# Four groups of in-place sums moved from a doubled loop into the product behind it

## The chip, the cores and the metric

The kernel runs on one core of a Trainium2 chip. The metric is the device time in microseconds (us) of one execution; the median of several runs is compared.

## What is computed

One decoder layer on a residual stream x of 1024 rows by 1024 columns in float32: a mixer (differential attention beside a short convolution, one projection in, one out), a layer norm, and a gated feed-forward part with a hidden width of 2816, with a second layer norm at the end. The part that matters here is the last product, the down projection, and its layer norm:

```python
def conv_glu(x, w_up, conv_w, conv_b, w_down):
    up = jnp.einsum('bsd,df->bsf', x, w_up)
    g, val = up[..., :D_FF], up[..., D_FF:]
    g = causal_dwconv(g, conv_w) + conv_b
    return jnp.einsum('bsf,fd->bsd', jax.nn.silu(g) * val, w_down)
...
        f = conv_glu(h, ffn_w_up[l], ffn_conv_w[l], ffn_conv_b[l], ffn_w_down[l])
        h = layer_norm(DEEPNORM_ALPHA * h + f, ln2_g[l], ln2_b[l])
```

## The kernel before

Every float32 operand of a matmul is split into a high part and a remainder. ScalarE casts the high part (L60), VectorE subtracts it from the operand (L61), and TensorE makes three products of 128x128 by 128x512: high by high (L69), high by low (L70), low by high (L71). In the trace the activations' operand is S and the weights' operand is T.

The down projection multiplies 1024 x 2816 activations by 2816 x 1024 weights. Both are cut in two along each side, and seven products of half blocks take the place of eight; sums of blocks are formed before some of the products. One product has 11 slices of the hidden width (HK = 11) and four blocks of 128 rows, so one slice is 4 x 3 = 12 matmuls, called a step here. X (dx in the trace) and Z (dz) are four accumulators each.

The order of the work:

1. The doubled loop, `for j in range(HK + 2)`, makes two products at once. At each j it does slice j of a11 by b11 into X, and slice j - 2 of (a21 + a22) by (b12 - b11) into Z. The two sums for Z are made by `add` (L802, on VectorE) into temporary tiles tm. When X is complete, `first_add` (L808) brings its four row blocks into the residual r11 (rw in the trace).
2. In the same loop, from j = 3 on, `thirds(j - 3)` overwrites four tiles of slice j - 3 with the sums that later products want: a21 becomes a11 - a21, a11 becomes a22 - a21 (the new one), b12 becomes b22 - b12, b11 becomes b12 + b11. These are four `add` of 128x512 on VectorE, also L802. The call for slice 10 stands behind the loop.
3. The third product, `product(X, a11, b11, ...)`, multiplies the new a11 and b11 into X. `product` makes the operands of slice i, then its 12 matmuls, then calls `after[i]` if there is one, then, for i in 0 and 1, two of the jobs in `owed` (here `first_add` of Z into r22, four in all).
4. Four more products follow in the same way, then the layer norm of the last rows.

The operand tiles S and T come from a ring of seven tiles, so a cast into a tile of the ring waits until the matmuls of the tile's former contents are over. The instructions of an engine run in the order in which the program puts them on that engine; that order is set when the program is built, it mostly follows the text, and an instruction whose inputs are ready early can stand ahead of one that is written before it.

Of the kernel before, what the change touches and what calls it, by code (L numbers as in the profile page):

```python
# [31 lines left out]
NEARLY = 4  # L32
FIN = 5
OWED = (0, 1)
POOL_LO = (2, 3, 4, 5, 6)
REUSE = 2
RMS_AT = [(c, 1) for c in range(4)]
# [6 lines left out]
def layer_kernel(ctx: ExitStack, tc: tile.TileContext, x, xt, w_in, w_v, lam, vecs, w_out, ln, w_up, w_down, out):  # L44
# [461 lines left out]
    def bank(name):  # L506
        return p8.tile([P, 512], F32, name=name, tag="b", bufs=8)
# [61 lines left out]
    def weights(t0, k, eng):  # L569
        raw = e0.tile([P, D], F32, name=f"wo{t0}_{k}_r", tag="wg", bufs=NWG)  # L570
        SQ.dma_start(raw, w_out[k * P:(k + 1) * P, :])
        wo = [e0.tile([P, 2, 512], F32R, name=f"wo{t0}_{k}_{d}", tag="ring", bufs=RING[0]) for d in range(2)]
        for d in range(2):
            split(wo[d][:, 0, :], wo[d][:, 1, :], raw[:, d * 512:(d + 1) * 512], eng=eng)
        return wo

    pending, late, held = [], [], {}
    for t0 in (0, 3, 6):
# [4 lines left out]
        for ki, k in enumerate(order):  # L583
            if ki < REUSE and t0:
                wo = held[k]
            else:
                wo = weights(t0, k, G if ki in POOL_LO and t0 == 6 else None)
            held[k] = wo
# [49 lines left out]
    def wgate(f):  # L638
        return wload8(f, "wg", NWG)
# [3 lines left out]
    for f in range(NEARLY):  # L643
        if f >= NEARLY - 2:
            turn(*rows_[f - NEARLY + 2])
        wg, X, Y = wgate(f), bank(f"X{f}"), bank(f"Y{f}")
# [19 lines left out]
    HK = NF // 2  # L666
# [4 lines left out]
    def operand(src, which, i, tail=False, eng=None):  # L671
        if tail and not (which == "T" and i < HK - NTAIL + RT):
            v = ep.tile([P, 2, 512], F32R, name=f"{which}{i}", tag="ra", bufs=NF - NKEEP)
        else:
            v = e0.tile([P, 2, 512], F32R, name=f"{which}{i}", tag="ring", bufs=RING[0])
        split(v[:, 0, :], v[:, 1, :], src, eng=eng)
        return v

    act, b11, ready = [], [], []
    for f in range(NF):  # L680
        if f in early:
            wg, X, c11 = early[f]
        else:
            wg, X, c11 = wgate(f), bank(f"X{f}"), None
# [69 lines left out]
    a11, a21 = [act[k][:, c0] for k in half1], [act[k][:, c1] for k in half1]  # L754
    a12, a22 = [act[k][:, c0] for k in half2], [act[k][:, c1] for k in half2]

    def residual(half, cols_, tiles):
        for t in range(4):
            SQ.dma_start(tiles[t], h1_d[4 * half + t][:, cols_])
        return tiles  # L760

    def rtiles(name, tag, bufs):
        return [ep.tile([P, 512], F32, name=f"{name}_{t}", tag=tag, bufs=bufs) for t in range(4)]
# [3 lines left out]
    def mm_row(ps, op, t, first, last):  # L767
        s_, t_ = op
        ts = slice(t * P, (t + 1) * P)
        mm3(ps[t], s_[:, 0, ts], s_[:, 1, ts], t_[:, 0, :], t_[:, 1, :], first, last, skip_group_check=True)  # L770

    def product(ps, sa, tb, first, ntail=0, done=None, after={}, prompt=False):
        ops = []

        def mms(i, t):
            mm_row(ps, ops[i], t, first and i == 0, i == HK - 1)
            if i == HK - 1:
                if ntail or prompt:
                    done(t)
                else:  # L780
                    owed.append(lambda: done(t))

        for i in range(HK):
            tail = i >= HK - ntail
            ops.append((operand(sa(i), "S", i, tail), operand(tb(i), "T", i, tail)))
            if not tail:
                for t in range(4):
                    mms(i, t)
            if i in after:
                after[i]()  # L790
            if i in OWED:
                for _ in range(2):
                    if owed:
                        owed.pop(0)()
        for t in range(4):
            for i in range(HK - ntail, HK):
                mms(i, t)

    def add(x_, y_, op, out=None):
        if out is None:  # L800
            out = ep.tile([P, 512], F32, name="tm", tag="r", bufs=4)
        V.tensor_tensor(out, x_, y_, op=op)  # L802
        return out
# [3 lines left out]
    def first_add(r, ps):  # L807
        return lambda t: V.scalar_tensor_tensor(r[t], r[t], ALPHA, ps[t], op0=ALU.mult, op1=ALU.add)  # L808

    def finish(t, r0, r1):  # L810
        mv = e1.tile([P, 2], F32, name="mv", tag="mv", bufs=3)
        V.bn_aggr(mv, st[t])
        ve = e1.tile([P, 1], F32, name="ve", tag="ve", bufs=3)
        G.tensor_scalar(ve, mv[:, 1:2], EPS, None, op0=ALU.add)
        rs = e1.tile([P, 1], F32, name="rs", tag="rs", bufs=3)
        G.tensor_tensor(rs, ve, mhalf, op=ALU.pow)
        for r, g, c in ((r0, g2[0], c0), (r1, g2[1], c1)):
            V.scalar_tensor_tensor(r, r, mv[:, 0:1], g, op0=ALU.subtract, op1=ALU.mult)
        for r, bb, c in ((r0, b2[0], c0), (r1, b2[1], c1)):
            V.scalar_tensor_tensor(r, r, rs, bb, op0=ALU.mult, op1=ALU.add)  # L820
            SQ.dma_start(out[t * P:(t + 1) * P, c], r)

    X = [bank(f"dx{t}") for t in range(4)]
# [3 lines left out]
    r22 = residual(1, c1, [r[:, 1, :] for r in rw])  # L827


    def thirds(i):  # L830
        add(a11[i], a21[i], ALU.subtract, a21[i])
        add(a22[i], a21[i], ALU.subtract, a11[i])
        add(b22[i], b12[i], ALU.subtract, b12[i])
        add(b12[i], b11[i], ALU.add, b11[i])

    for j in range(HK + 2):
        if j < HK:
            op = ready.pop(0) if ready else (operand(a11[j], "S", j), operand(b11[j], "T", j))
            for t in range(4):
                mm_row(X, op, t, j == 0, j == HK - 1)  # L840
        if j >= 2:
            i = j - 2
            op = (operand(add(a21[i], a22[i], ALU.add), "S", i),
                  operand(add(b12[i], b11[i], ALU.subtract), "T", i))
            for t in range(4):
                mm_row(Z, op, t, i == 0, i == HK - 1)
            if j >= HK:
                for t in (0, 1) if j == HK else (2, 3):
                    first_add(r11, X)(t)
        if j >= 3:  # L850
            thirds(j - 3)
    thirds(HK - 1)
    for t in range(4):
        owed.append(lambda t=t: first_add(r22, Z)(t))

    r12 = residual(0, c1, rtiles("r12", "r", 4))

    product(X, lambda i: a11[i], lambda i: b11[i], False, done=first_add(r12, X))

    def done_p3(t):  # L860
        V.tensor_tensor(r12[t], r12[t], Z[t], op=ALU.add)
# [17 lines left out]
    def done_p7(t):  # L879
# [4 lines left out]
            after={FIN + t: (lambda t=t: finish(t, r11[t], r12[t])) for t in range(4)})  # L884
# [51 lines left out]
```

## Time and profile before

| what | value |
|---|---|
| median of 3 runs | 1144.28 us |
| lowest of 3 runs | 1142.41 us |
| profiled execution, its time | 1145.87 us |
| profiled execution, its span | 1143.5 us |
| TensorE busy | 1090.8 us, 95% of the span |
| VectorE busy | 914.4 us, 80% |
| ScalarE busy | 522.5 us, 46% |
| granted TensorE clock, mean | 0.986 of full speed |
| doubled loop and third product on TensorE | 912.46 to 1015.02 us |

The highest of the three runs, 2755.74 us, stands alone; the median is not moved by it.

The times in the rows below are microseconds from the start of the span. In the rows PE is TensorE, PEld its weight load, DVE VectorE, ACT ScalarE, POOL GpSimd. A matmul's duration reaches over the start of the next one, since they are pipelined; the pace is the distance of the starts. The same holds for the instructions of VectorE and ScalarE.

### The profile page before, as it was taken

How to read it: one execution, taken by the hardware profiler on the slowest of the kernel's cores; microseconds unless marked ns; L12 is line 12 of the kernel's file. 1: busy time of each engine (PE TensorE's matmuls, PEld its weight loads, DVE VectorE, ACT ScalarE, POOL GpSimd, SP SyncE). 2: the span in 40 equal slices, each digit the busy share in tenths (PEclk: the TensorE clock that was granted, in tenths of full speed). 3: DMA queues.
4: the chain of work that ended last, by engine and by line, in shares of the span. 5: the costliest groups of instructions: out<-in, count | busy, mean ns of one | idle time of the engine just before them, and what ended most of it. 6: DMA issues, size and time to landing. Idle time of an engine off the chain costs nothing.

```text
span 1143.5 us, 13823 instructions
## 1 busy us (share of the span) xinstructions
PE 1090.8 (95%) x4924; PEld 876.7 (77%) x4924; DVE 914.4 (80%) x1377; ACT 522.5 (46%) x980; POOL 174.6 (15%) x198
## 2 busy tenths in 40 slices
PE   7899999999999999789999999999999999899997
PEld 5676777877768888568888888888888887688885
DVE  7858889779887788998967676767677599977697
ACT  5347677377676334434433434343434243344450
POOL 4501313113032214760000000000000000000102
PEclk9899999999999999999999999999999999999999
DMA  7430121211205764423232222222222393111111
GB/s 257 136 111 26 42 82 41 86 60 47 79 28 172 263 203 164 152 74 111 94 109 75 92 74 93 74 93 73 93 74 74 121 411 139 37 62 40 38 74 73
DMA packets 50276, 118.51 MB, mean 104 GB/s; under 512 B 5024, under 2 KB 18464, under 8 KB 50208
## 3 DMA queue, kind: packets, MB, share of 16 engines
q1 hardware_dynamic: 50208, 117.64, 29.8%
q8 instruction: 38, 0.62, 0.2%
q14 instruction: 30, 0.25, 0.1%
HBM read 90.88 MB, written 26.74 MB: 103 GB/s over the span
## 4 chain that ended last, share of the span: by engine, by line
PE 67%; DVE 17%; ACT 6%; DMA 5%; POOL 3%; issue 2%; POOLq 0%; DVEq 0%; SPq 0%; ACTq 0%
PE X L71 8%; PE X L69 8%; PE X L70 8%; PE Z L70 5%; PE Z L71 5%; PE Z L69 5%; PE dx L70 3%; PE dx L71 3%; PE dx L69 3%; PE op L71 2%; PE op L70 2%; PE op L69 2%; DVE a L61 2%; PE dz L70 2%; PE dz L71 2%
## 5 line engine op out<-in xcount | busy, mean ns | idle before, releaser
L61 DVE TENSOR_TENSOR a<-s,a 128x512 fp32r<-128x512 f32 x118 | 85.4, 725 | 45.1 <-ACT a L60 44.1
L60 ACT CAST a<-s 128x512 fp32r<-128x512 f32 x118 | 73.4, 623 | 94.8 <-PE X L71 42.7
L60 ACT CAST a<-w 128x512 fp32r<-128x512 f32 x106 | 66.0, 623 | 87.4 <-PE X L71 40.7
L61 DVE TENSOR_TENSOR a<-w,a 128x512 fp32r<-128x512 f32 x102 | 71.4, 701 | 21.6 <-ACT a L60 21.2
L60 ACT CAST T<-b 128x512 fp32r<-128x512 f32 x66 | 40.7, 622 | 72.1 <-PE dz L71 35.6
L70 PE MATMUL dx<-T,S 128*128 128x512 f32 x176 | 69.8, 397 | 3.6 <-DVE T L61 3.6
L71 PE MATMUL dx<-T,S 128*128 128x512 f32 x176 | 69.4, 395 | 0.0
L69 PE MATMUL dx<-T,S 128*128 128x512 f32 x176 | 67.3, 390 | 0.0
L61 DVE TENSOR_TENSOR T<-b,T 128x512 fp32r<-128x512 f32 x66 | 45.4, 690 | 24.1 <-ACT T L60 24.1
L687 POOL MEMSET gs<- 128x2 f32 x22 | 2.2, 100 | 379.2 <-DVE t L706 379.2
L71 PE MATMUL op<-wo,cl 128*128 128x512 f32 x128 | 51.4, 402 | 4.5 <-DVE cl L61 4.5
L422 DVE TENSOR_REDUCE nm<-sc 128x1 f32<-128x128 f32 (+5 forms) x64 | 47.6, 751 | 7.6 <-PE sc L421 7.1
L69 PE MATMUL dz<-T,S 128*128 128x512 f32 x132 | 49.2, 401 | 3.8 <-ACT T L60 3.7
L70 PE MATMUL dz<-T,S 128*128 128x512 f32 x132 | 52.2, 396 | 0.0
L71 PE MATMUL dz<-T,S 128*128 128x512 f32 x132 | 51.9, 393 | 0.0
L69 PE MATMUL op<-wo,ch 128*128 128x512 f32 x128 | 51.4, 402 | 0.0
L70 PE MATMUL op<-wo,ch 128*128 128x512 f32 x128 | 51.0, 399 | 0.0
L426 ACT ACTIVATE p<-sc,nm 128x128 f32<-128x128 f32 (+5 forms) x64 | 47.6, 746 | 7.3 <-DVE p L435 4.1
L707 ACT ACTIVATE t<-t 128x1024 f32<-128x1024 f32 x22 | 23.4, 1062 | 51.2 <-DVE t L706 51.2
L344 POOL TENSOR_TENSOR me<-me,y 128x256 f32<-128x256 f32 x16 | 12.6, 786 | 217.9 <-ACT y L343 217.9
L419 PE MATMUL sc<-k,q 128*128 128x512 f32 (+2 forms) x96 | 37.2, 394 | 7.3 <-ACT p L426 6.1
L60 ACT CAST wo<-wo_r 128x512 fp32r<-128x512 f32 x40 | 24.4, 620 | 41.0 <-PE op L71 37.8
(312 smaller groups left out, 3415.3 us busy)
## 6 DMA issues: line engine op xcount, KB each, us to landing
w<-in_w_up SPq DMA_DIRECT2D x44, 512.0 KB, 3.3
b<-in_w_down SPq DMA_DIRECT2D x44, 256.0 KB, 6.8
w<-in_w_in SPq DMA_DIRECT2D x20, 512.0 KB, 3.5
wo_r<-in_w_out SPq DMA_DIRECT2D x20, 512.0 KB, 5.4
act_d<-act SPq DMA_DIRECT2D x19, 512.0 KB, 2.6
ra<-act_d SPq DMA_DIRECT2D x19, 512.0 KB, 7.1
v_d<-vs SPq DMA_DIRECT2D x16, 256.0 KB, 2.7
vhl<-v_d SPq DMA_DIRECT2D x8, 512.0 KB, 4.7
```

The lines of the kernel that those rows point to most:

```text
L60: A.copy(hi, src)
L61: (eng or V).tensor_tensor(lo, src, hi.bitcast(F32), op=ALU.subtract)
L69: T.matmul(ps, lh, rh, start=first, stop=False, **kw)
L70: T.matmul(ps, lh, rl, start=False, stop=False, **kw)
L71: T.matmul(ps, ll, rh, start=False, stop=last, **kw)
L344: G.tensor_tensor(me, me, y, op=ALU.mult)
L419: T.matmul(sc[:, bs], q2[m][:, qs], k2[m][:, bs], start=True, stop=False)
L422: V.tensor_reduce(nm[:, m:m + 1], sc[:, :n], axis=AX.X, op=ALU.max, negate=True)
L426: A.activation(pt[:, :n], sc[:, :n], AF.Exp, bias=nm[:, m:m + 1], accum_out=sm[:, m:m + 1])
L687: G.memset(gs[:, 0:2], 0.0)
L707: A.activation(t_, t_, AF.Silu)
```

## The change

The call of `thirds` in the doubled loop is limited to slices 0 to 6. Those of slices 7, 8, 9 and 10 are given to the third product as `after`, behind its steps 0, 2, 4 and 6. What is computed is the same.

```diff
+NTHIRD = 7
...
     def thirds(i):
         add(a11[i], a21[i], ALU.subtract, a21[i])
         add(a22[i], a21[i], ALU.subtract, a11[i])
...
-        if j >= 3:
+        if 3 <= j < NTHIRD + 3:
             thirds(j - 3)
-    thirds(HK - 1)
     for t in range(4):
         owed.append(lambda t=t: first_add(r22, Z)(t))
 
     r12 = residual(0, c1, rtiles("r12", "r", 4))
 
-    product(X, lambda i: a11[i], lambda i: b11[i], False, done=first_add(r12, X))
+    product(X, lambda i: a11[i], lambda i: b11[i], False, done=first_add(r12, X),
+            after={2 * i: (lambda i=i: thirds(NTHIRD + i)) for i in range(HK - NTHIRD)})
```

## Rows read from the trace of the kernel before

**Rows 1.** The page, first part: busy time, share and instructions of each engine.

```profile
PE 1090.8 (95%) x4924; PEld 876.7 (77%) x4924; DVE 914.4 (80%) x1377; ACT 522.5 (46%) x980; POOL 174.6 (15%) x198
```

**Rows 2.** Windows: busy time of each engine by stage, granted clock, DMA share, GB/s.

```profile
core 0: us, PE busy (x) PEld busy (x) DVE busy (x) ACT busy (x) POOL busy (x), PEclk, DMA share, GB/s
915.00:985.00 70.00, 62.58 (x260) 48.98 (x259) 69.59 (x116) 27.14 (x48) 0.00 (x0) 0.97 0.61 239
985.00:1015.00 30.00, 30.00 (x128) 24.66 (x127) 24.73 (x41) 11.43 (x20) 0.00 (x0) 0.95 0.03 10
1015.00:1045.00 30.00, 30.00 (x134) 24.83 (x133) 23.18 (x39) 12.56 (x22) 0.00 (x0) 1.00 0.27 87
1045.00:1075.00 30.00, 30.00 (x134) 24.86 (x133) 18.82 (x31) 12.58 (x22) 0.00 (x0) 1.00 0.04 12
1075.00:1105.00 30.00, 30.00 (x134) 24.60 (x133) 29.54 (x52) 18.62 (x33) 5.72 (x8) 1.00 0.26 94
```

**Rows 3.** Waits, 900 to 1020, TensorE: total us, times, longest us.

```profile
PE dz L69 <- ACT T L60: 3.7, 2, 2.2
PE dx L70 <- DVE T L61: 3.6, 1, 3.6
```

**Rows 4.** Timeline, TensorE: start, us, instruction, count, idle before and its releaser.

```profile
912.46 0.39 PE L69 MATMUL dx<-T,S 128*128 128x512 f32 x1
...
967.94 0.39 PE L71 MATMUL dz<-T,S 128*128 128x512 f32 x1
970.56 1.97 PE L69 MATMUL dz<-T,S 128*128 128x512 f32 x4 [2.23 <-ACT T L60]
...
976.58 1.20 PE L69 MATMUL dz<-T,S 128*128 128x512 f32 x4 [1.42 <-ACT T L60]
...
979.80 0.84 PE L69 MATMUL dx<-T,S 128*128 128x512 f32 x3
984.27 0.74 PE L70 MATMUL dx<-T,S 128*128 128x512 f32 x1 [3.64 <-DVE T L61]
...
987.79 0.39 PE L69 MATMUL dx<-T,S 128*128 128x512 f32 x1
...
1015.02 0.39 PE L69 MATMUL dz<-T,S 128*128 128x512 f32 x1
...
1134.98 0.39 PE L71 MATMUL dx<-T,S 128*128 128x512 f32 x1
```

**Rows 5.** Timeline, VectorE, around the moved sums (966.08: group 7; 982.32: end of 10).

```profile
965.48 0.69 DVE L61 TENSOR_TENSOR T<-tm,T 128x512 fp32r<-128x512 f32 x1
966.08 0.70 DVE L802 TENSOR_TENSOR ra<-ra 128x512 f32<-128x512 f32 x1
...
968.49 0.70 DVE L802 TENSOR_TENSOR tm<-ra,ra 128x512 f32<-128x512 f32 x1
969.09 0.69 DVE L802 TENSOR_TENSOR tm<-b,b 128x512 f32<-128x512 f32 x1
969.69 0.69 DVE L808 SCALAR_TENSOR_TENSOR rw<-rw,dx 128x512 f32<-128x512 f32 x1
...
982.32 0.70 DVE L802 TENSOR_TENSOR b<-b,b 128x512 f32<-128x512 f32 x1
982.92 0.70 DVE L61 TENSOR_TENSOR S<-act,S 128x512 fp32r<-128x512 f32 x1
983.52 0.70 DVE L61 TENSOR_TENSOR T<-b,T 128x512 fp32r<-128x512 f32 x1
984.12 1.30 DVE L808 SCALAR_TENSOR_TENSOR rw<-rw,dz 128x512 f32<-128x512 f32 x2
...
990.72 0.70 DVE L802 TENSOR_TENSOR act<-ra,act 128x512 f32<-128x512 f32 x1
```

**Rows 6.** Timeline, ScalarE: two casts and what they waited for.

```profile
969.22 0.62 ACT L60 CAST S<-tm 128x512 fp32r<-128x512 f32 x1 [4.12 <-DVE tm L802]
...
980.00 0.62 ACT L60 CAST T<-b 128x512 fp32r<-128x512 f32 x1 [0.87 <-PE dz L71]
```

## The prediction

> **What bounds the kernel now.** The page's first part gives TensorE 95% of the span and VectorE 80% [rows 1]: TensorE is the bound as a mean, and the question is where it is not. The windows by stage answer it [rows 2]. In the doubled loop (915 to 985) VectorE is busy 69.59 of 70.00 us and TensorE only 62.58; in the third product (985 to 1015) TensorE is busy all 30.00 and VectorE 24.73. So the loop is paced by VectorE and what follows it by TensorE. The waits of TensorE say the same: its pauses end on a cast (L60) that had waited for VectorE, or on a remainder of VectorE itself (L61) [rows 3].
>
> How much TensorE loses there comes from its timeline [rows 4]. From 987.79 on the third product runs without a pause: 120 matmuls up to 1015.02, 27.23 us, so 0.227 us each and 2.72 us for a step (one slice, 12 matmuls). The 33 steps of X, Z and the third product begin at 912.46; without loss they would end at 912.46 + 33 x 2.723 = 1002.3. They end at 1015.0, so **12.7 us are lost**: pauses of 2.23, 1.42 and 3.64 us, two stretches in which matmuls are slower right after a pause (eight from 984.27 to 987.79 take 3.52 instead of 1.81 us, 1.7 lost; four L69 at 970.56 take 1.97 instead of the 1.20 at 976.58, and that stretch loses about as much), and about 2 us of small waits. From 1015.02 the other four products are 44 steps, 119.8 us, up to 1134.8; the last matmul starts at 1134.98 [rows 4]. After the third product nothing is lost, and whatever it ends earlier the end should be earlier too.
>
> **What the change moves.** Groups 7 to 10 of the in-place sums, four sums each, leave the loop and stand behind steps 0, 2, 4 and 6 of the third product. No instruction is added or removed. In the trace group 7 holds VectorE from 966.08 to the next instruction at 968.49 [rows 5]: 2.41 us, 0.602 a sum. The four groups are 16 sums, **9.6 us**. The first begins at 966.08 and the last, the sixteenth, at 982.32, all ahead of the low parts of the third product's first slice, for which TensorE waits 3.64 us. The sums issue no transfer, so no DMA and nothing in SP's queue moves. They do not use ScalarE or GpSimd.
>
> **The loop after the change.** Up to 965.48 nothing differs. Then I let VectorE's instructions follow in the order of the trace, 0.60 us each. The two sums for Z's slice 9 start at 966.08 and 966.68 instead of 968.49 and 969.09, X's first residual fills the place that it fills now, the remainders start at 967.88 and 968.48. A cast begins 0.04 us after its sum has ended (968.49 + 0.69 to 969.22) [rows 5, 6], so the casts are over at 967.4 and 968.0. Slice 8 of Z leaves TensorE at 968.2, slice 9 can begin at once; its low part is there at 969.25 (0.2 us late), it ends at 971.1. Slice 10: sums at 969.68 and 970.28, casts over at 971.0 and 971.6, TensorE begins at 971.7 and gets the low part at 972.85, so it waits 0.6 and 0.25 and ends at 974.7. Without loss this would be 972.4: the loop still loses 2.3 us, half of it before 968 where nothing changes. Both slow stretches go with the pauses ahead of them.
>
> **The third product after the change.** VectorE does the last residual of X at 972.68, then the remainders of slice 0 at 973.28 and 973.88: TensorE goes from the loop into step 0 without a pause, up to 977.4. Now program order puts group 7 (974.5 to 976.9), two residuals of Z, remainders of slice 1 (978.08 and 978.68), two residuals, slice 2 (980.48 and 981.08), group 8 (to 984.1), slices 3 and 4, group 9, slices 5 and 6, group 10, slice 7. Today the residuals stand between slices 0 and 1 in just this way (984.12) [rows 5]. Where TensorE is short of a low part it does the four high products of the step first (the rows L69 x4), 0.9 us. So step 1 begins at 977.4, has its four high products done at 978.3 and waits for the low part until 979.45: **1.2 us**. Step 2 does not wait (981.85 against 982.2). Step 3 waits from 984.9 to 985.45: **0.6 us**. From step 4 on VectorE is ahead, since two steps want 4 remainders and one group, 4.8 us, in 5.44 us of TensorE. The casts are no limit: T's third slice waits for Z's last matmul, as now at 980.00 [rows 6], and each later one for the step three before it. Steps 4 to 10 run through, 987.3 + 19.1 = 1006.3.
>
> **The sum:** 1015.0 - 1006.3 = **8.7 us gained**; 2.3 + 1.2 + 0.6 = 4.1 of the 12.7 lost remain. The profiled execution took 1145.87 us with a span of 1143.5, so 1137.2 and 1134.8 after; the runs' median is 1144.28, 1.6 below that execution, and 1144.28 - 8.7 = **1135.6**.
>
> Costed at nothing: the 11 sums for the next product, with which VectorE now fills its free time from 990.7 on [rows 5], start later, about 997. The cover is the free time behind: VectorE is busy 23.18 of 30 us in the next stage and 18.82 of 30 in the one after it [rows 2], 18 us free, against 9.6 us moved. The stage from 1075 has no room (29.54 of 30); if it had to take all of the 9.6 us, the gain would be gone, but 18 us of room lie ahead of it. The last product's sums (L802 on b) follow in the same free time.
>
> Bounds of what the trace does not show. The order inside the third product: if the remainders of slices 1 and 3 come ahead of the groups, both waits fall away, gain 10.4; if TensorE takes the matmuls by row instead of the high products first, each wait starts 0.7 us earlier, gain 8.0. Nothing lost at all would be 12.7. I take program order with the high products first, because both stand so in the rows of now.
>
> **Does TensorE's clock fall in the new pauses?** After the pause of 1.42 us before 976.58 the matmuls are at full speed (2.4 GHz), after those of 2.23 and 3.64 us at half (1.2 GHz) [rows 4]. My longest pause, 1.2 us, is below the first, so I count nothing. The Trainium skill (TensorE: Matmul & The Clock Gate, A second HAM failure mode: psum-queue depth-cycling) says that frequent short idle gaps between groups of matmuls can make the clock go back and forth, and that throughput is lost at each return. The pause of 976.58 does not bear it out here; by that rule the sum would be 7.0.
>
> **The rivals.**
> 1. The clock falls once in the third product. For it: waits of 1.2 and 0.6 us lie 4 us apart, behind 0.6 in the loop. Against it: the row at 976.58. Price 1.7 us (the eight matmuls from 984.27): 7.0 gained, 1137.3; with both waits longer by 0.7, 5.6, 1138.7. Chance 0.15.
> 2. The change does not do what it says: VectorE's order is not strictly that of the text (X's residual of 969.69 stands ahead of remainders that are written before it), and the moved sums could fill the loop's gaps again. For it: their inputs are ready in the loop. Against it: in the rows of now group 7 stands in its place, behind the remainder of 965.48 [rows 5], and a gap between sum and remainder takes one instruction that the residuals already fill. If three of four groups stay in the loop, 9.6 / 4 = 2.4 us gained, 1141.9; chance 0.07.
> 3. Slower: VectorE paces the third product. Each of the four groups stands in front of remainders that TensorE wants next; if every one stalls it in full and the clock falls each time, that is 4 x (2.41 + 1.7) = 16.4 against 12.7 - 2.3 = 10.4 won in the loop: 6.0 slower, 1150.3. It decides from 10.4 us of pauses on. Against it: 4.8 us of work for 5.44 us, and casts that may run three steps ahead. Chance 0.04.
>
> The forecast with its own range (8.0 to 12.7 gained, 1131.6 to 1136.3) has 0.74. Undisturbed single times lie 1.9 below and 1.6 above the median; with that at both ends, and with rival 1 taken in (1131.6 - 1.9 and 1138.7 + 1.6), the range is 1129.7 to 1140.3, and leaves out rivals 2 and 3 and little more. A measurement of this kernel can tell about 2% (23 us) from no change. All that is lost in the stage is 12.7 us, so no case reaches 2% faster, and the slower rival gives 0.5%: faster 0.01, within 2% 0.97, slower 0.02.
>
> **What would show it.** Right: the third product's last matmul ends near 1006 and all later rows are some 9 us earlier; the half-speed matmuls near 970 and 984 are gone; 16 sums stand between the third product's remainders. Wrong step: a pause over 2 us in the third product with half-speed matmuls behind it (rival 1); sums of groups 7 to 10 ahead of slice 0's remainders (rival 2); pauses in steps 1, 3, 5 and 7 (rival 3); pauses from 1060 on would mean that the room behind did not cover the moved work.

## The result, and the profile after

The changed kernel takes 1134.02 us (median of 4 runs, 1133.13 to 1136.27) against 1144.03 us before; the ratio is 0.992, with a 95% interval of 0.9899 to 0.9941. A second measurement, the run `after_again` below, gives 1134.32 us (6 runs) against 1143.32 us, ratio 0.9926, interval 0.9914 to 0.9937. So the change saves 9 to 10 us. It is clear of zero and far inside 2%. The profiled execution took 1134.1 us, its span is 1132.3 us.

The change shifts the lines of the code by one: L70, L71 and L72 are now the three matmuls (high by high, high by low, low by high), L61 the cast, L62 the remainder, L803 the sums and L809 the residuals.

The windows of the changed kernel, by the same stages as [rows 2] (columns as there):

```profile
915.00:985.00 70.00, 68.30 (x291) 53.46 (x290) 69.97 (x117) 29.19 (x52) 0.00 (x0) 1.00 0.57 224
985.00:1015.00 30.00, 30.00 (x134) 24.82 (x133) 29.84 (x51) 12.63 (x23) 0.00 (x0) 1.00 0.14 45
1015.00:1045.00 30.00, 30.00 (x134) 24.86 (x133) 23.52 (x39) 12.65 (x23) 0.00 (x0) 1.00 0.16 53
1045.00:1075.00 30.00, 30.00 (x134) 24.85 (x133) 20.49 (x36) 14.84 (x27) 3.30 (x5) 1.00 0.11 36
1075.00:1105.00 30.00, 30.00 (x132) 24.35 (x131) 30.00 (x50) 15.05 (x27) 2.42 (x4) 1.00 0.18 70
```

From 915 to 985 TensorE is busy 68.30 us instead of 62.58 and makes 291 matmuls instead of 260, at full granted clock (1.00, before 0.97), while VectorE is as busy as it was. The third product has moved ahead, so groups 7 and 8 now lie just before 985 (971.86 to 981.47) and groups 9 and 10 behind it; from 985 to 1015 VectorE is busy 29.84 us instead of 24.73, and TensorE does not pause there.

The waits of TensorE, 900 to 1130, changed kernel (total us, times, longest us), beside [rows 3]:

```profile
PE dx L71 <- DVE T L62: 1.2, 2, 0.9
PE dz L70 <- ACT T L61: 0.4, 1, 0.4
```

And its timeline, the rows that answer to [rows 4]:

```profile
909.82 0.39 PE L70 MATMUL dx<-T,S 128*128 128x512 f32 x1
...
965.53 1.17 PE L70 MATMUL dz<-T,S 128*128 128x512 f32 x4
...
969.12 1.21 PE L70 MATMUL dz<-T,S 128*128 128x512 f32 x4 [0.42 <-ACT T L61]
...
972.37 0.39 PE L70 MATMUL dx<-T,S 128*128 128x512 f32 x1
...
974.86 1.07 PE L70 MATMUL dx<-T,S 128*128 128x512 f32 x4
976.81 0.50 PE L71 MATMUL dx<-T,S 128*128 128x512 f32 x1 [0.88 <-DVE T L62]
...
978.76 1.07 PE L70 MATMUL dx<-T,S 128*128 128x512 f32 x4
...
981.48 1.07 PE L70 MATMUL dx<-T,S 128*128 128x512 f32 x4
982.82 0.50 PE L71 MATMUL dx<-T,S 128*128 128x512 f32 x1 [0.28 <-DVE T L62]
...
984.80 0.39 PE L70 MATMUL dx<-T,S 128*128 128x512 f32 x1
...
1003.85 0.39 PE L70 MATMUL dz<-T,S 128*128 128x512 f32 x1
...
1123.81 0.39 PE L72 MATMUL dx<-T,S 128*128 128x512 f32 x1
```

The measure used from here on is **the stretch**: from X's first matmul (909.82) to the first matmul of the product behind the third one (1003.85). It was 1015.02 - 912.46 = 102.56 us [rows 4] and is 94.03 us: 8.5 us shorter. Without any loss it would be 33 x 2.723 = 89.9 us. From its end to the last matmul it is 119.96 us in both. The remaining 2.64 us between the two profiles (912.46 against 909.82) lie ahead of the first instruction that the change touches; TensorE's order up to there is the same in both programs. Most of it arises in the first 300 us, where TensorE makes 1325 matmuls (0.227 us each) before and 1335 after.

### The profile page after: what moved, and what is told of

Its sections match the earlier page's. It is cut to its first block, busy times and chain, and to the rows that moved or that the text cites. A ratio compares the mean times of both kernels' runs of the same rounds, so it can differ in the third digit from the quotient of the medians.

```text
span 1132.3 us, 13828 instructions
## 1 busy us (share of the span) xinstructions
PE 1084.2 (96%) x4924; PEld 870.9 (77%) x4924; DVE 913.2 (81%) x1377; ACT 522.1 (46%) x980; POOL 174.4 (15%) x198
## 4 chain that ended last, share of the span: by engine, by line
PE 66%; DVE 18%; ACT 6%; DMA 4%; POOL 4%; issue 2%; SPq 0%; POOLq 0%; DVEq 0%; ACTq 0%
PE X L70 8%; PE X L72 8%; PE X L71 8%; PE Z L72 5%; PE Z L71 5%; PE Z L70 5%; PE dx L71 2%; PE dx L72 2%; PE dx L70 2%; PE op L70 2%; PE op L72 2%; PE op L71 2%; DVE a L62 2%; PE dz L70 2%; PE dz L71 2%
## 5 line engine op out<-in xcount | busy, mean ns | idle before, releaser
L62 DVE TENSOR_TENSOR a<-s,a 128x512 fp32r<-128x512 f32 x118 | 85.3, 724 | 45.2 <-ACT a L61 44.2
L61 ACT CAST a<-s 128x512 fp32r<-128x512 f32 x118 | 73.4, 623 | 94.5 <-PE X L72 40.0
L61 ACT CAST a<-w 128x512 fp32r<-128x512 f32 x106 | 65.9, 623 | 87.1 <-PE X L72 40.8
L62 DVE TENSOR_TENSOR a<-w,a 128x512 fp32r<-128x512 f32 x102 | 72.3, 709 | 20.4 <-ACT a L61 20.0
L61 ACT CAST T<-b 128x512 fp32r<-128x512 f32 x66 | 40.6, 622 | 68.4 <-PE dz L72 34.0
L71 PE MATMUL dx<-T,S 128*128 128x512 f32 x176 | 69.1, 392 | 1.2 <-DVE T L62 1.2
L72 PE MATMUL dx<-T,S 128*128 128x512 f32 x176 | 68.5, 389 | 0.0
L70 PE MATMUL dx<-T,S 128*128 128x512 f32 x176 | 66.0, 390 | 0.0
L62 DVE TENSOR_TENSOR T<-b,T 128x512 fp32r<-128x512 f32 x66 | 45.2, 687 | 16.6 <-ACT T L61 16.6
L72 PE MATMUL op<-wo,cl 128*128 128x512 f32 x128 | 51.0, 398 | 5.7 <-DVE cl L62 5.7
L71 PE MATMUL dz<-T,S 128*128 128x512 f32 x132 | 51.8, 393 | 0.0
L72 PE MATMUL dz<-T,S 128*128 128x512 f32 x132 | 51.4, 390 | 0.0
L70 PE MATMUL op<-wo,ch 128*128 128x512 f32 x128 | 51.1, 399 | 0.0
L71 PE MATMUL op<-wo,ch 128*128 128x512 f32 x128 | 50.5, 395 | 0.0
L70 PE MATMUL dz<-T,S 128*128 128x512 f32 x132 | 48.4, 394 | 0.5 <-ACT T L61 0.4
L61 ACT CAST wo<-wo_r 128x512 fp32r<-128x512 f32 x40 | 24.4, 619 | 40.4 <-PE op L72 37.8
```

Source lines behind the costliest of these rows:

```text
L61: A.copy(hi, src)
L62: (eng or V).tensor_tensor(lo, src, hi.bitcast(F32), op=ALU.subtract)
L70: T.matmul(ps, lh, rh, start=first, stop=False, **kw)
L71: T.matmul(ps, lh, rl, start=False, stop=False, **kw)
L72: T.matmul(ps, ll, rh, start=False, stop=last, **kw)
```

## The experiments

The theory: the amount of work that VectorE has to do ahead of the next low part sets the time in the loop and at the start of the third product. TensorE loses what VectorE is late, and after a long pause some more, because it comes back at half speed. The rivals: the gain goes with the number of sums moved; the clock alone makes it; the third product has room for any amount; VectorE's load can be cut in any way one likes. All experiments start from the changed kernel.

| kernel | groups moved, behind which steps | stretch, us | median us (runs) | ratio to before, 95% interval |
|---|---|---|---|---|
| before | none | 102.56 | 1143.2 (19, beside e1 to e4) | |
| after | 7 to 10, behind 0, 2, 4, 6 | 94.03 | 1134.02 (4) | 0.992, 0.9899 to 0.9941 |
| after_again | the same | 93.99 | 1134.32 (6) | 0.9926, 0.9914 to 0.9937 |
| e1_two_groups | 9, 10, behind 0, 2 | 98.84 | 1139.27 (10) | 0.9966, 0.9956 to 0.9977 |
| e2_late | 7 to 10, behind 2, 3, 5, 6 | 92.76 | 1133.8 (4) | 0.992, 0.99 to 0.9941 |
| e3_six_groups | 5 to 10, behind 0 to 5 | 94.27 | 1135.62 (4) | 0.9932, 0.9912 to 0.9953 |
| e4_two_at_0 | 7 to 10, behind 0, 0, 4, 6 | 97.30 | 1138.97 (10) | 0.9959, 0.9949 to 0.9969 |
| e5_left_out | 7 to 10 not made | 92.21 | 1132.65 (1) | |
| e6_b_sums_pool | as after, sums on b by GpSimd | 108.63 | 1150.31 (4) | 1.0065, 1.0048 to 1.0082 |
| e7_five_spread | 6 to 10, behind 2, 3, 5, 6, 7 | 90.48 | 1131.7 (5) | 0.9907, 0.9892 to 0.9921 |

**e1_two_groups: only half of the groups.**

```diff
-NTHIRD = 7
+NTHIRD = 9
```

> Only groups 9 and 10 are moved (behind steps 0 and 2 of the third product). Measure: the stretch from X's first matmul to the first matmul of the product behind the third one, 102.56 us before, 94.03 us after, 89.9 without loss. Theory (VectorE's work ahead of the low parts that TensorE wants next sets the time): the loop loses what it lost before up to slice 10 of Z, the pause of 3.64 us and the half-speed matmuls behind it go, and waits of about 1.5 and 0.6 us come in steps 1 and 3: 99.3 us. If the gain went simply with the number of groups moved, half of 8.5: 98.3 us. If the clock alone made the gain (one of two half-speed stretches gone, 1.7 us): 100.9 us.

Measured: 98.84 us, between the theory's 99.3 and the proportional 98.3, and away from the clock's 100.9. The stretch alone does not tell the first two apart; the rows do. TensorE's timeline of e1:

```profile
967.79 1.21 PE L70 MATMUL dz<-T,S 128*128 128x512 f32 x4 [2.22 <-ACT T L61]
968.87 0.63 PE L71 MATMUL dz<-T,S 128*128 128x512 f32 x1
...
973.80 1.19 PE L70 MATMUL dz<-T,S 128*128 128x512 f32 x4 [1.32 <-ACT T L61]
...
981.49 0.50 PE L71 MATMUL dx<-T,S 128*128 128x512 f32 x1 [0.93 <-DVE T L62]
...
987.51 0.50 PE L71 MATMUL dx<-T,S 128*128 128x512 f32 x1 [0.24 <-DVE T L62]
```

Groups 7 and 8 are still in the loop, and both of the pauses behind them are still there, 2.22 and 1.32 us (2.23 and 1.42 before [rows 4]), with the half-speed matmuls (0.63 us) behind the first. The pause of 3.64 us, which stood behind groups 9 and 10, is gone. In the third product the two short pauses appear in steps 1 and 3, as the theory puts them; with 0.93 and 0.24 us they are shorter than the 1.5 and 0.6 that were expected. The loop is as long as before (67.1 us to the last matmul of Z in both), so the whole gain lies in the third product. So each pause belongs to the groups that stand in front of it.

**e2_late: the same four groups, later in the third product.**

```diff
-            after={2 * i: (lambda i=i: thirds(NTHIRD + i)) for i in range(HK - NTHIRD)})
+            after={k: (lambda i=i: thirds(i)) for k, i in ((2, 7), (3, 8), (5, 9), (6, 10))})
```

> The same four groups moved, but behind steps 2, 3, 5 and 6 instead of 0, 2, 4 and 6. Theory: the waits of 0.88 us in step 1 and 0.28 us in step 3 come from groups 7 and 8 that stand ahead of remainders; with the groups later VectorE has slack ahead of each (12.0 us of work for 12.3 us up to step 4, 20.4 for 20.4 up to step 7), so the stretch falls from 94.03 to about 92.9 us. Rival: VectorE has no slack and the waits only move to later steps: 94.0 us.

Measured: 92.76 us. TensorE's waits, 900 to 1040, of e2, with no other row:

```profile
PE dz L70 <- ACT T L61: 0.6, 2, 0.4
```

The third product does not wait for VectorE any more; its two pauses, and the slower matmuls right behind them, cost 1.3 us. They did not move elsewhere. The time, 1133.8 us, cannot be told from the changed kernel's 1134.02: 1.3 us is 0.1%.

**e3_six_groups: more moved work.**

```diff
-NTHIRD = 7
+NTHIRD = 5
...
-            after={2 * i: (lambda i=i: thirds(NTHIRD + i)) for i in range(HK - NTHIRD)})
+            after={i: (lambda i=i: thirds(NTHIRD + i)) for i in range(HK - NTHIRD)})
```

> Six groups moved (5 to 10, behind steps 0 to 5). Theory: the loop's last losses go (some 2 us), but VectorE then paces steps 2 to 6 of the third product with 3.6 us a step against TensorE's 2.7, waits of about 0.9 us in each, 4.9 us in all: the stretch is about 95 us, longer than with four. Rival: the third product has room for any of them and only the loop's gain counts: 92 us.

Measured: 94.27 us, near the theory's 95 and not the rival's 92. TensorE's waits, 900 to 1030, and rows of its timeline, e3:

```profile
PE dx L71 <- DVE T L62: 2.3, 4, 0.6
```

```profile
979.66 0.50 PE L71 MATMUL dx<-T,S 128*128 128x512 f32 x1 [0.60 <-DVE T L62]
...
983.27 0.50 PE L71 MATMUL dx<-T,S 128*128 128x512 f32 x1 [0.56 <-DVE T L62]
...
986.88 0.50 PE L71 MATMUL dx<-T,S 128*128 128x512 f32 x1 [0.56 <-DVE T L62]
...
990.50 0.50 PE L71 MATMUL dx<-T,S 128*128 128x512 f32 x1 [0.58 <-DVE T L62]
```

The four pauses are 3.61, 3.61 and 3.62 us apart. That is the time of four sums and two remainders on VectorE, 6 x 0.602 us, and not TensorE's 2.72: VectorE paces these steps. What six groups win in the loop they lose again behind it: the loop is 1.8 us shorter than with four groups, the third product 2.1 us longer. The idle time of each pause is 0.6 us, but the matmuls beside it are spaced wider too: a paced step takes 3.6 us, 0.9 more than TensorE's 2.72, which is the loss that was expected for a step. There are four such steps, not five; that is why the stretch is under the forecast of 95. This is the third rival of the prediction, seen from its own side: with two groups more it begins to hold.

**e4_two_at_0: one long pause instead of a short one.**

```diff
-            after={2 * i: (lambda i=i: thirds(NTHIRD + i)) for i in range(HK - NTHIRD)})
+            after={0: lambda: (thirds(7), thirds(8)), 4: lambda: thirds(9), 6: lambda: thirds(10)})
```

> Four groups moved, but group 8 stands directly behind group 7 after step 0 (so after steps 0, 0, 4, 6). It makes one longer pause in step 1: 0.88 + 2.41 = 3.3 us instead of 0.88. If a pause of that length lets TensorE's clock fall as those of 2.23 and 3.64 us did before: the stretch is 94.03 + 2.41 + 1.7 - 0.28 = 97.9 us, with half-speed matmuls behind the pause. If the clock stays: 96.2 us.

Measured: 97.30 us. TensorE's timeline of e4 around step 1:

```profile
977.02 1.07 PE L70 MATMUL dx<-T,S 128*128 128x512 f32 x4
981.40 0.80 PE L71 MATMUL dx<-T,S 128*128 128x512 f32 x1 [3.31 <-DVE T L62]
981.99 0.63 PE L72 MATMUL dx<-T,S 128*128 128x512 f32 x1
...
984.55 0.42 PE L72 MATMUL dx<-T,S 128*128 128x512 f32 x1
984.81 0.40 PE L70 MATMUL dx<-T,S 128*128 128x512 f32 x1
```

The pause is 3.31 us, as expected, and the matmuls behind it take 0.63 us instead of 0.39: half speed, so the clock falls (granted clock 0.50 from 981.40 to 984.00). The eight from 981.40 to 984.81 take 3.41 us; in the changed kernel the same eight take 1.95 (976.81 to 978.76). The pause is 2.43 us longer and the slow matmuls take 1.46 more. Step 3 has no wait any more; in the changed kernel it takes 981.48 to 984.80, 3.32 us instead of 2.72, so 0.60 go. That makes 3.29; the stretch is 3.27 longer. The order of the same 16 sums alone is worth more than a third of what the change gains.

**e5_left_out: the floor.**

```diff
-            after={2 * i: (lambda i=i: thirds(NTHIRD + i)) for i in range(HK - NTHIRD)})
+            after={})
```

> Groups 7 to 10 of the in-place sums are left out altogether (16 of the 44 sums are not made). It is the floor of what any other place for them can give. Theory: the loop's small losses stay, the waits of 0.88 and 0.28 us in the third product go: the stretch from X's first matmul to the first of the product behind the third is 92.7 us against 94.03. If the moved sums cost more than those two waits: under 92 us.

Measured: 92.21 us, 1.8 us under the changed kernel and 0.5 under e2. It leaves out sums that the products need, so it is no kernel to use, only a floor for other places of these four groups; it is a single run. In their new place the 16 sums cost 1.8 us of the 9.6 us that VectorE spends on them; the rest is covered by TensorE's work. The stretch is 0.5 us under the forecast because that took off only the idle time of the two waits, 0.88 and 0.28 us. From the end of the loop, with the one matmul that it makes ahead, the third product takes 29.92 us here (972.28 to 1002.20), which is 11 x 2.72 without any loss, and 31.71 in the changed kernel (972.14 to 1003.85): the waits cost 1.8 us with the wider spaced matmuls behind them. What is left of loss, 2.4 us, lies in the loop.

**e6_b_sums_pool: half of all the in-place sums on GpSimd.**

```diff
-        add(b22[i], b12[i], ALU.subtract, b12[i])
-        add(b12[i], b11[i], ALU.add, b11[i])
+        G.tensor_tensor(b12[i], b22[i], b12[i], op=ALU.subtract)
+        G.tensor_tensor(b11[i], b12[i], b11[i], op=ALU.add)
```

> The changed kernel with the two sums on b of every group (22 of 44) made on GpSimd instead of VectorE. GpSimd is idle in this stretch; its nearest row is 0.786 us for 128x256, so some 1.5 us for a sum of 128x512 and 33 us in all. Theory that VectorE's load alone sets the loop: 8.4 us of load go from the loop and 4.8 from the third product, the stretch falls to 91 to 92.5 us and the kernel becomes 1.5 to 3 us faster than with the change alone. Rival: the two engines slow each other on these 128x512 sums, VectorE's 0.60 us grows, and the stretch stays or becomes longer (97 us or more).

Measured: 108.63 us, and 1150.31 us for the kernel, slower than before. The theory in its simple form, VectorE's load alone, fell. GpSimd's timeline in e6, then VectorE's at the same time:

```profile
919.51 11.08 POOL L835 TENSOR_TENSOR b<-b,b 128x512 f32<-128x512 f32 x1 [26.70 <-DMA b<-in_w_down]
930.67 1.64 POOL L836 TENSOR_TENSOR b<-b,b 128x512 f32<-128x512 f32 x1
932.27 1.74 POOL L835 TENSOR_TENSOR b<-b,b 128x512 f32<-128x512 f32 x1
...
940.82 1.60 POOL L836 TENSOR_TENSOR b<-b,b 128x512 f32<-128x512 f32 x1
944.38 1.68 POOL L835 TENSOR_TENSOR b<-b,b 128x512 f32<-128x512 f32 x1 [1.96 <-DVE tm L803]
...
972.85 1.67 POOL L835 TENSOR_TENSOR b<-b,b 128x512 f32<-128x512 f32 x1 [3.77 <-DVE tm L803]
...
983.60 1.61 POOL L836 TENSOR_TENSOR b<-b,b 128x512 f32<-128x512 f32 x1
```

```profile
928.75 0.69 DVE L803 TENSOR_TENSOR tm<-ra,ra 128x512 f32<-128x512 f32 x1
929.47 1.67 DVE L803 TENSOR_TENSOR ra<-ra 128x512 f32<-128x512 f32 x1
931.06 1.80 DVE L803 TENSOR_TENSOR tm<-b,b 128x512 f32<-128x512 f32 x1
932.78 1.78 DVE L62 TENSOR_TENSOR S<-tm,S 128x512 fp32r<-128x512 f32 x1
...
941.21 1.76 DVE L803 TENSOR_TENSOR tm<-ra,ra 128x512 f32<-128x512 f32 x1
943.00 0.69 DVE L803 TENSOR_TENSOR ra<-ra 128x512 f32<-128x512 f32 x1
...
973.29 0.68 DVE L809 SCALAR_TENSOR_TENSOR rw<-rw,dx 128x512 f32<-128x512 f32 x1
```

From 929.47 on, VectorE's instructions start about 1.7 us apart instead of 0.60, one for each sum of GpSimd (1.60 to 1.74 us), and they are back at 0.69 us when GpSimd stops at 942.4. GpSimd's first sum lasts 11.08 us, while VectorE goes on at its own pace up to 929.47. So the two do not run side by side; one waits for the other. A sum given to GpSimd takes 1.1 us of VectorE's time where it saves 0.6. By the Trainium skill (SBUF — State Buffer, Who interferes with whom) a VectorE instruction with two inputs in SBUF contends with a GpSimd instruction that reads SBUF, because its second input comes through the read interface that the two engines share. The trace agrees: the slow rows are sums and remainders with two inputs in SBUF, while the residual at 973.29, which takes one input from an accumulator of TensorE, needs 0.68 us in the middle of a GpSimd sum (972.85 to 974.52). The longest pause of TensorE that follows is 3.83 us, for a remainder in the loop.

e6 changes the place of work as well as its engine. All 22 sums of GpSimd lie between 919.51 and 985.21, ahead of the third product, those of groups 7 to 10 among them: half of the moved work came back into the loop. An estimate from the two prices, 22 x 1.1 - 14 x 0.6 = 15.8 us more in the loop, is near the measured 16.4; the third product loses nothing. What GpSimd would cost with these eight sums in the third product was not run.

**e7_five_spread: what the others point to.** One group more than the change moves, each placed where VectorE has slack, and Z's four residuals, for which nothing waits soon, put off.

```diff
-NTHIRD = 7
+NTHIRD = 6
...
-    def product(ps, sa, tb, first, ntail=0, done=None, after={}, prompt=False):
+    def product(ps, sa, tb, first, ntail=0, done=None, after={}, prompt=False, owed_at=OWED):
...
-            if i in OWED:
+            if i in owed_at:
...
-            after={2 * i: (lambda i=i: thirds(NTHIRD + i)) for i in range(HK - NTHIRD)})
+            after={k: (lambda i=i: thirds(i)) for k, i in ((2, 6), (3, 7), (5, 8), (6, 9), (7, 10))}, owed_at=(8, 9))
```

> Five groups moved (6 to 10), behind steps 2, 3, 5, 6 and 7 of the third product, and Z's four residuals, which nothing waits for until that product ends, behind steps 8 and 9 instead of 0 and 1. Theory (VectorE's work in front of each low part sets the time): up to step 7 VectorE has 8 x 1.2 + 4 x 2.41 = 19.2 us of work ahead of slice 7's low part for which TensorE leaves 20.4, so the third product does not wait, and the loop loses 2.4 us of VectorE work more, which takes most of its last 2.9 us of loss: the stretch is 90.5 to 91 us (94.03 with the change, 92.75 with the four groups placed later). Rival: the loop's last losses come from the cast behind each sum and not from VectorE's load: the stretch stays at 92 us or above.

Measured: 90.48 us, 0.6 us above what is possible without any loss. TensorE has no pause between 900 and 1030. The window of the loop in e7:

```profile
915.00:985.00 70.00, 70.00 (x307) 57.01 (x306) 69.97 (x117) 30.55 (x54) 0.00 (x0) 1.00 0.58 227
```

Both engines are full: TensorE makes 307 matmuls from 915 to 985, where it made 260 before and 291 with the change. Of the 2.28 us that the stretch is shorter than in e2, 1.75 come from the loop, where one group less stands; 0.53 come from the third product, which loses nothing any more (29.92 us). What the later residuals and the new places each give of that was not run apart. The kernel takes 1131.7 us, 2.6 us under `after_again` on the same chip. Their intervals against before, 0.9892 to 0.9921 and 0.9914 to 0.9937, overlap by a little, so the times alone do not settle that e7 is the faster one; the stretch, 3.5 us shorter, speaks for it.

**after_again: the change once more.** The file is the changed kernel, without an edit.

> The changed kernel once more, beside the version above on the same chip: a stretch of 94.0 us in the profile, and a time 10 us under that of before if the first measurement holds, 8.5 us if part of it was the front of the execution, where the two profiles differ by 2.6 us before any instruction that the change touches.

Measured: a stretch of 93.99 us (94.03 the first time) and 9.0 us under before, between the two expectations. X's first matmul stands at 908.68 here, at 909.82 in the first profile after, at 912.46 in that of before and at 912.00 in e4, with the same instructions up to there. A difference of a few us ahead of that point is therefore no effect of the change; e4 makes 1322 matmuls in its first 300 us, about as few as the 1325 of before.

## Why the prediction was right

- **What bounds the loop.** Right. VectorE is full in the loop in every version; with four groups less in it TensorE makes 31 matmuls more up to 985, and e1 shows that each pause goes with the groups in front of it.
- **The loop after the change.** 2.3 us of loss were forecast. The third product follows from 972.37 on, with one of its matmuls made before; 972.37 - 0.23 - 909.82 = 62.3 us against 22 x 2.723 = 59.9 is a loss of 2.4. The wait ahead of Z's slice 10 is 0.42 us where 0.6 was forecast.
- **The third product after the change.** VectorE's order was forecast as slice 0, group 7, two residuals, slice 1, two residuals, slice 2, group 8. The trace has it so. VectorE's timeline of the changed kernel, beside [rows 5]:

```profile
971.25 0.69 DVE L62 TENSOR_TENSOR T<-b,T 128x512 fp32r<-128x512 f32 x1
971.86 0.69 DVE L803 TENSOR_TENSOR ra<-ra 128x512 f32<-128x512 f32 x1
...
973.66 0.69 DVE L803 TENSOR_TENSOR b<-b,b 128x512 f32<-128x512 f32 x1
974.26 1.28 DVE L809 SCALAR_TENSOR_TENSOR rw<-rw,dz 128x512 f32<-128x512 f32 x2
975.46 0.69 DVE L62 TENSOR_TENSOR S<-act,S 128x512 fp32r<-128x512 f32 x1
976.06 0.69 DVE L62 TENSOR_TENSOR T<-b,T 128x512 fp32r<-128x512 f32 x1
...
995.32 1.29 DVE L803 TENSOR_TENSOR act<-ra,act 128x512 f32<-128x512 f32 x2
```

The low part of slice 1 starts at 976.06; with the 2.64 us of the front that is 978.70, and 978.68 was forecast. The waits were forecast in steps 1 and 3, with 1.2 and 0.6 us; they are there, with 0.88 and 0.28. The forecast counted a wait from the pace of the four high products, the profile from their modelled end, and the first matmul behind each wait is followed at a wider distance (976.81 to 977.14). With both, the third product loses 31.71 - 29.95 = 1.8 us, as forecast. In all 94.03 - 89.86 = 4.2 us of the loss are left, and 4.1 were forecast. The high products came first (974.86 x4, 981.48 x4), so the other order among the bounds did not arise; its price stands in two sums of the prediction that do not agree, 0.7 us once in the gain of 8.0 and twice in rival 1's 5.6.

- **The sum.** 8.7 us were forecast, the stretch gives 8.5. The median was forecast as 1135.6 us and is 1134.02 and 1134.32; the medians differ by 9 to 10 us. What they have beyond 8.5 is within what the front of the execution adds or takes, which differs by almost 4 us between profiles of the same instructions. In the nine measurements of the table, the gain of the median is between 1.2 us less and 1.5 us more than the gain of the stretch; why the front differs stays open.
- **What was costed at nothing.** The sums for the next product start at 995.32, 997.96 with the front added, and about 997 was forecast. The stages behind take them up: from the stretch's end to the last matmul it is 119.96 us before and after.
- **Rival 1, the clock.** It did not fall: the matmuls behind the pauses of 0.88 and 0.28 us are at full speed (granted clock 1.00 from 974 to 985). The rule of the Trainium skill (TensorE: Matmul & The Clock Gate, A second HAM failure mode: psum-queue depth-cycling) is not borne out by pauses of this length. e4 shows the price had they been longer: by the prediction's count, eight matmuls against 1.81 us, it is 3.41 - 1.81 = 1.6 us on top of the pause, where 1.7 was reckoned.
- **Rivals 2 and 3.** No sum of groups 7 to 10 stands ahead of slice 0's remainders (971.25, then 971.86), so the change does what it says. VectorE does not pace the third product with four groups; e3 shows that it begins to with six.

## What to carry to other kernels

Where an engine that feeds TensorE is full in one stage and has room in the next, work that only the later stage needs is worth moving, and the gain can be read off beforehand by following the two engines instruction by instruction past the moved work. How that work is placed among the low parts that TensorE wants next decides what it costs in its new stage: the same 16 sums gave stretches of 92.76, 94.03 and 97.30 us. For each step, set the work that stands in front of what the step needs against the time that TensorE leaves for it, and put off first the work for which nothing waits.

## What the runs showed of the hardware that was not expected

- VectorE and GpSimd hold each other up on sums of 128x512 with both inputs in SBUF: VectorE needs 0.60 us from start to start alone and about 1.7 us while GpSimd makes sums of 1.6 to 1.7 us, and GpSimd's first sum lasted 11.08 us while VectorE ran on. An idle GpSimd was no free helper for a full VectorE.
- TensorE's clock after the pauses of these stretches: after 0.24 to 1.77 us (1.77 in e6) all matmuls were at full speed. After 2.22 us (e1) four still were (1.21 us for the four) and only the next ones at half, while after 2.23 us (before) the first four already took 1.97. After 3.31 us (e4), 3.64 us (before) and 3.83 us (e6) the first ones were slower at once.
